# The first layer's gate, shift and scale computed by tiles of 128 features, between the phases of the second scan

## The chip, the cores and the metric

The kernel runs on one core of a Trainium2 chip. The metric is the time of one execution on the device in microseconds (us): the median of several runs. A profile is taken of one further execution; its trace has every instruction with its start, its end and what it waited for. TensorE (PE) multiplies matrices, a stationary operand being loaded first (PEld) and a moving operand then passing through; DVE, ACT and POOL work elementwise; SP issues the DMA transfers. Each engine takes its instructions in the order in which they are written for it.

## What is computed

Two layers of a diffusion backbone for 1024 latent and 128 context tokens, each 1024 wide. Each layer modulates its tokens by six vectors that are projected from a conditioning vector; there are two conditioning vectors, one for the latent and one for the context tokens.

```python
sh1, sc1, g1, sh2, sc2, g2 = jnp.split(jax.nn.silu(cvec) @ lp['w_ada'] + lp['b_ada'], 6, axis=-1)
h = rmsnorm(x, lp['g_pre_mix']) * (1.0 + sc1) + sh1
m, extras = mixing(h, lp, ctx)
x = x + g1 * rmsnorm(m, lp['g_post_mix'])
h = rmsnorm(x, lp['g_pre_ffn']) * (1.0 + sc2) + sh2
f = conv_ffn(h, lp['w_up'], lp['ffn_conv_w'], lp['ffn_conv_b'], lp['w_down'])
x = x + g2 * rmsnorm(f, lp['g_post_ffn'])
```

The change concerns three of the six parts in the first layer: part 2, the gate `g1`, and parts 3 and 4, shift `sh2` and scale `sc2` of the feed-forward sub-layer. Each is a product of two vectors of 1024 with a 1024x1024 fp32 matrix, plus a bias. `mixing` splits into a convolution module (conformer), a gated DeltaNet with four heads (two scans over nine chunks of 128 tokens, heads 0 and 1 in the first, 2 and 3 in the second) and a neighbourhood attention with four heads; their outputs are concatenated and projected.

## The kernel before

One program, written out without loops on the chip, runs layer 0 and then layer 1. In a layer it runs, in this order: the dense products of DeltaNet heads 0 and 1 and their first scan; the dense products and block inversions (line 820) of heads 2 and 3; the attention's dense products and the products of `z` (`z_dense`, line 600); the second scan, with pieces of the attention between its phases; `gdn_out` (transposes, line 998); what is left of the attention, the conformer's output (`conf_out`, lines 1067 and 1098) and the split of the output projection's weights (`out_weights`); the output projection with the next normalisation (`out_proj`, transposes on line 387); the feed-forward stage; and the normalisation for the next layer.

The six vectors are made in different places. Parts 0 and 1 of layer 0 come first of all (`ada_pe`). Part 5 of layer 0 and all six of layer 1 are made inside the feed-forward stage of layer 0 (`ada`, its products on line 241 with a 128x128 stationary operand and 64 columns). Parts 2, 3 and 4 of layer 0 are made by `ada_fill`: the stationary operand is `self.cs[:, k, :]`, two columns (the two conditioning vectors after silu), and rows of the weight matrix, 512 wide, are the moving operand (line 273). The bias comes as one more product of one row (line 278). The result lies on two partitions. For the gate it is multiplied by `g_post_mix` and written to `rows` in DRAM (lines 284 and 285), where `out_proj` reads it; for shift and scale it is copied by ACT, turned by small transposes (line 291) and copied to `mod`, features on partitions, which `turn` reads. The gate is run as a whole after the attention's dense products; shift and scale are stepped one product at a time with the rest of the attention after the second scan, from a pool `adf` of their own.

For most of the kernel a planner sets each engine's order from the order of the program, as soon as it holds an instruction to be ready. In the second scan and `gdn_out` TensorE's order is that of the program (`manual_schedule(engines=ENG)`); the other engines' is planned. `gdn_scan` runs the phases of two heads in turn and calls `fill` twice in each of nine steps; `fill` takes pieces of the attention until their stated costs reach `FILL` = 2.2:

```python
            go(0)
            if s:
                go(1)
            go(0)
            fill(s)
            go(1)
            go(0)
            go(1)
            fill(s)
```

A phase of the scan uses PSUM banks "a" and, one for each head, "b" or "c". Lines 930 (state products), 938, 949 and 951 are the scan's, 1307 (scores), 1335 (transposes, "turns") and 1351 (values) the attention's; their pieces have stated costs of 0.6, 0.55 and 0.6. Weight buffers `raw`, `whi` and `wlo` have two slots each; the attention's bias tiles of heads 0 and 2 take one slot of `whi` and of `wlo`. Line 624 loads rows that are 512 bytes long for 128 partitions, line 271 the weights of the projections.

Of the kernel before, what the change touches and what calls it, by code (L numbers as in the profile page):

```python
# [9 lines left out]
F32 = mybir.dt.float32  # L10
# [3 lines left out]
ALU = mybir.AluOpType  # L14
# [94 lines left out]
class K:  # L109
# [141 lines left out]
    def ada_fill(self, l, part, tag, both, pool=None):  # L251

        nc, I = self.nc, self.I
        def raw():
            if pool:
                return pool.tile([128, 512], F32, tag="adf", name="rawa", bufs=6)
            self.cnt += 1
            if self.cnt % 3 == 0:
                return self.wp.tile([128, 1024], F32, tag="raw", name="rawa", bufs=self.rawb)
            return self.wp.tile([128, 4 * TAIL], F32, tag=("whi", "wlo")[self.cnt % 3 - 1], name="rawa", bufs=self.wb)  # L260

        if part != 2:
            m = self.cp.tile([128, 2, KT], F32, tag=f"mod{part}", name="mod", bufs=2)
            self.mod[l, part] = m
        for ns in ((0, 1),) if both else ((0,), (1,)):
            w = 512 * len(ns)
            c0 = 512 * ns[0]
            pss = [self.psum(tag) for n in ns]
            for k in range(KT):
                r = raw()  # L270
                nc.sync.dma_start(out=r[:, :w], in_=I["w_ada"][l, 128 * k:128 * k + 128, part * D + c0:part * D + c0 + w])
                for i, ps in enumerate(pss):
                    nc.tensor.matmul(ps[0:2, :], self.cs[:, k, :], r[:, 512 * i:512 * i + 512], start=(k == 0), stop=False)  # L273
                yield
            r = raw()
            nc.sync.dma_start(out=r[0:1, :w], in_=I["b_ada"][l:l + 1, part * D + c0:part * D + c0 + w])
            for i, ps in enumerate(pss):
                nc.tensor.matmul(ps[0:2, :], self.ones[0:1, 0:2], r[0:1, 512 * i:512 * i + 512], start=False, stop=True)
            x = raw()
            if part == 2:  # L280
                nc.sync.dma_start(out=x[0:2, :w], in_=I["g_post_mix"][l:l + 1, c0:c0 + w].to_broadcast([2, w]))
                for i, ps in enumerate(pss):
                    c = slice(512 * i, 512 * i + 512)
                    nc.vector.tensor_tensor(out=x[0:2, c], in0=ps[0:2, :], in1=x[0:2, c], op=ALU.mult)
                nc.sync.dma_start(out=self.rows[l, part][:, c0:c0 + w], in_=x[0:2, :w])
            else:
                for i, (n, ps) in enumerate(zip(ns, pss)):
                    self.act(x[0:2, 512 * i:512 * i + 512], ps[0:2, :], AF.Copy)
                    for k in range(4):
                        c = 512 * i + 128 * k  # L290
                        nc.tensor.transpose(ps[:, 2 * k:2 * k + 2], x[0:2, c:c + 128], self.ident[0:2, 0:2])
                    pv = ps[:, 0:8].rearrange("p (k s) -> p s k", s=2)
                    mo = m[:, :, 4 * n:4 * n + 4]
                    if part == 4:
                        g = self.v(l, "g_pre_ffn", 4 * n, 4).unsqueeze(1).to_broadcast([128, 2, 4])
                        self.stt(mo, pv, 1.0, g, ALU.add, ALU.mult)
                    else:
                        nc.vector.tensor_copy(out=mo, in_=pv)
            yield
# [1331 lines left out]
    def run(self):  # L1631
# [23 lines left out]
        for l in range(L):  # L1655
# [53 lines left out]
            if l == 0:  # L1709
                run(self.ada_fill(0, 2, "d", True))  # L1710
# [149 lines left out]
```

## Time and profile before

| | us |
|---|---|
| median of 3 runs | 3434.82 |
| lowest and highest run | 3434.27 and 3440.16 |
| the profiled execution | 3428.76 |
| its span, first to last instruction | 3426.6 |
| TensorE busy | 3182.8 |
| DVE, ACT, POOL busy | 2094.5, 1323.0, 1151.5 |

The span is that of the traced instructions. "Busy" counts the time in which an engine has an instruction at work; matmuls overlap, so the distance between the starts of two says what one costs in a row of them. One fp32 product appears as two instructions in the trace. Rows of line numbers read: line, engine, operation, result<-operands, count, duration in ns (least, median, most), first and last start in us from the span's start.

### The profile page before, as it was taken

The numbers are of one execution on the slowest core, as the hardware profiler recorded it, in microseconds if no ns is written. First come the engines' busy times: TensorE is split into PE (matmuls) and PEld (weight loads), VectorE is DVE, ScalarE is ACT, GpSimd is POOL, SyncE is SP. The second block draws the span as 40 slices with busy tenths as digits, with TensorE's granted clock in tenths as the row PEclk, the third lists the DMA queues.
The fourth block names the chain that finished last, engine by engine and source line by source line (L and its number), as shares of the span: only waits on it lengthen the run. The fifth ranks groups of instructions, "written<-read, shape, count | busy, mean of one in ns | idle before, by whom it ended". The sixth has DMA issues, their size and how long they took to land.

```text
span 3426.6 us, 51062 instructions
## 1 busy us (share of the span) xinstructions
PE 3182.8 (93%) x19072; PEld 2874.3 (84%) x19072; DVE 2094.5 (61%) x3952; ACT 1323.0 (39%) x2987; POOL 1151.5 (34%) x1125
## 2 busy tenths in 40 slices
PE   7998888889999999999989988878799999999997
PEld 4898886737889899989978988877588999999997
DVE  3576997644566656655475769986554444444446
ACT  4335524644533333333254345246553222222223
POOL 2423223424544434434235233244342222221114
PEclk9999999999999999999999999989899999999999
DMA  5422444265322222222144224432541111111113
GB/s 190 119 64 77 139 135 127 68 221 165 108 82 83 86 72 77 87 74 71 41 141 133 68 79 139 134 93 60 178 153 45 41 43 53 43 44 38 37 37 135
DMA packets 243085, 323.78 MB, mean 94 GB/s; under 512 B 76175, under 2 KB 169631, under 8 KB 241750
## 3 DMA queue, kind: packets, MB, share of 16 engines
q1 hardware_dynamic: 242838, 320.52, 30.7%
q8 instruction: 151, 2.47, 0.3%
q14 instruction: 96, 0.79, 0.1%
HBM read 252.85 MB, written 67.59 MB: 94 GB/s over the span
## 4 chain that ended last, share of the span: by engine, by line
PE 59%; DVE 8%; DMA 4%; POOL 3%; issue 2%; ACT 2%; SPq 1%; DVEq 0%; POOLq 0%; ACTq 0%
PE d L429 18%; PE d L431 18%; PE d L430 18%; DVE cu L119 1%; PE a L930 1%; DVE adacc L119 1%; PE a L387 1%; DVE cv L119 1%; DVE XN L1625 1%; PE b L273 1%; DVE F L1626 0%; PE a L820 0%; PE S L1307 0%; PE c L241 0%; DVE keys L1626 0%
## 5 line engine op out<-in xcount | busy, mean ns | idle before, releaser
L431 PE MATMUL d<-hhi,wlo 128*128 128x386 f32 (+1 forms) x3072 | 1059.0, 345 | 14.9 <-POOL wlo L420 14.9
L429 PE MATMUL d<-hhi,whi 128*128 128x386 f32 (+1 forms) x3072 | 1055.3, 344 | 6.4 <-DVE cv L119 6.4
L430 PE MATMUL d<-hlo,whi 128*128 128x386 f32 (+1 forms) x3072 | 1055.2, 343 | 0.0
L420 POOL TENSOR_TENSOR wlo<-raw,whi 128x1024 fp32r<-128x1024 f32 x136 | 348.7, 2566 | 1064.7 <-ACT whi L116 1063.1
L119 DVE SCALAR_TENSOR_TENSOR cv<-d,fvec,cv 128x384 f32<-128x384 f32 (+1 forms) x528 | 325.3, 617 | 462.0 <-ACT cv L116 453.5
L431 PEld LDWEIGHTS d<-hhi,wlo 128*128 128x128 f32 x3072 | 585.6, 191 | 17.9 <-POOL wlo L420 16.4
L429 PEld LDWEIGHTS d<-hhi,whi 128*128 128x128 f32 x3072 | 587.6, 191 | 10.7 <-issue 8.8
L430 PEld LDWEIGHTS d<-hlo,whi 128*128 128x128 f32 x3072 | 588.0, 191 | 2.7 <-issue 0.7
L1539 DVE TENSOR_TENSOR f<-d,f 128x512 f32<-128x512 f32 x360 | 245.1, 687 | 163.7 <-PE d L431 161.9
L116 ACT ACTIVATE cv<-d,fvec 128x384 f32<-128x384 f32 (+1 forms) x264 | 174.7, 663 | 439.9 <-PE d L431 431.4
L429 PE MATMUL d<-wdh,ahi 128*128 128x512 f32 x792 | 315.6, 398 | 10.9 <-DVE f L1539 8.4
L430 PE MATMUL d<-wdl,ahi 128*128 128x512 f32 x792 | 313.4, 396 | 0.0
L431 PE MATMUL d<-wdh,alo 128*128 128x512 f32 x792 | 312.5, 395 | 0.0
L119 DVE SCALAR_TENSOR_TENSOR cu<-cu,vec 128x292 f32<-128x292 f32 (+1 forms) x480 | 248.2, 559 | 1.9
L116 ACT ACTIVATE whi<-raw 128x1024 fp32r<-128x1024 f32 x136 | 144.2, 1060 | 175.7 <-PE d L430 124.3
L223 POOL TENSOR_TENSOR adacc<-adacc,adpr 128x512 f32<-128x512 f32 x112 | 152.6, 1362 | 125.4 <-ACT adpr L116 94.8
L429 PEld LDWEIGHTS d<-wdh,ahi 128*128 128x128 f32 x792 | 149.0, 188 | 50.0 <-DVE f L1539 13.1
L1526 POOL TENSOR_TENSOR wdl<-rawd,wdh 128x512 fp32r<-128x512 f32 x88 | 118.7, 1349 | 184.3 <-ACT wdh L116 183.8
L431 PEld LDWEIGHTS d<-wdh,alo 128*128 128x128 f32 x792 | 148.7, 188 | 36.1 <-issue 0.7
L430 PEld LDWEIGHTS d<-wdl,ahi 128*128 128x128 f32 x792 | 148.9, 188 | 34.4 <-issue 1.4
L116 ACT ACTIVATE adpr<-adraw,cs 128x512 f32<-128x512 f32 x112 | 81.0, 723 | 240.9 <-POOL adacc L223 191.5
L1515 DVE TENSOR_TENSOR alo<-sg,ahi 128x384 fp32r<-128x384 f32 x132 | 110.8, 840 | 69.5 <-ACT ahi L116 69.2
(381 smaller groups left out, 5199.1 us busy)
## 6 DMA issues: line engine op xcount, KB each, us to landing
raw<-in_w_up_t SPq DMA_DIRECT2D x88, 512.0 KB
adraw<-in_w_ada SPq DMA_DIRECT2D x112, 256.0 KB
raw<-in_w_in_t SPq DMA_DIRECT2D x48, 512.0 KB
rawd<-in_w_down SPq DMA_DIRECT2D x88, 256.0 KB
xs<-x SPq DMA_DIRECT2D x27, 512.0 KB
x<-xs SPq DMA_DIRECT2D x27, 512.0 KB
rawa<-in_w_ada SPq DMA_DIRECT2D x24, 512.0 KB
x<-in_x SPq DMA_DIRECT2D x18, 512.0 KB
```

The source lines that it names most:

```text
L116: return self.nc.scalar.activation(out=out, in_=in_, func=func, **kw)
L119: return self.nc.vector.scalar_tensor_tensor(out=out, in0=in0, scalar=s, in1=in1, op0=op0, op1=op1, **kw)
L223: nc.gpsimd.tensor_tensor(out=acc[:, 1, :], in0=acc[:, 1, :], in1=pr, op=ALU.add)
L273: nc.tensor.matmul(ps[0:2, :], self.cs[:, k, :], r[:, 512 * i:512 * i + 512], start=(k == 0), stop=False)
L387: nc.tensor.transpose(ps[:, 128 * k:128 * k + 128], xn[:, 512 * g + 128 * k:512 * g + 128 * k + 128], self.ident)
L420: nc.gpsimd.tensor_tensor(out=lo[:, :n], in0=raw[:, :n], in1=hi[:, :n].bitcast(F32), op=ALU.subtract)
L429: nc.tensor.matmul(out, shi, mhi, start=(i == 0), stop=False)
L430: nc.tensor.matmul(out, shi, mlo, start=False, stop=False)
L431: nc.tensor.matmul(out, slo, mhi, start=False, stop=(i == n - 1))
L1515: nc.vector.tensor_tensor(out=lo[:, :n], in0=sg[:, :n], in1=hi[:, :n].bitcast(F32), op=ALU.subtract)
L1526: nc.gpsimd.tensor_tensor(out=lo, in0=raw[:, :512], in1=hi[:].bitcast(F32), op=ALU.subtract)
L1539: nc.vector.tensor_tensor(out=f[t][:, cs], in0=ps, in1=f[t][:, cs], op=ALU.add)
```

## The change

`ada_fill` goes and `ada_cols` takes its place. For each tile of 128 output features it loads all 1024 rows of 128 columns of the weight matrix (`r`, in runs of 512 bytes), makes them the stationary operand, eight 128x128 blocks one after another, and lets the two columns of `self.cs` pass. The result has features on partitions; ACT adds the bias and writes one column for each conditioning vector into `mod`. Loads run three tiles ahead (`la`). The gate is turned once at the end, multiplied by `g_post_mix` and written to `rows`; the scale gets its `g_pre_ffn` at its end. The generator has 25 steps: 24 tiles, and the turn of the gate. The run of the gate ahead of the second scan is taken out. In the second scan of layer 0 `fill` takes one step from its third call on, once its pieces have passed half of `FILL`, and counts it as 0.8; the steps use bank "c" in one call and "b" in the next. What is left of the steps is taken with the rest of the attention as before; the pool `adf` is gone.

```diff
--- before.py
+++ after.py
@@ -248,55 +248,48 @@
                     nc.vector.tensor_copy(out=m, in_=pv)
             yield
 
-    def ada_fill(self, l, part, tag, both, pool=None):
+    def ada_cols(self, l, parts, la=3):
 
         nc, I = self.nc, self.I
+
         def raw():
-            if pool:
-                return pool.tile([128, 512], F32, tag="adf", name="rawa", bufs=6)
             self.cnt += 1
             if self.cnt % 3 == 0:
                 return self.wp.tile([128, 1024], F32, tag="raw", name="rawa", bufs=self.rawb)
-            return self.wp.tile([128, 4 * TAIL], F32, tag=("whi", "wlo")[self.cnt % 3 - 1], name="rawa", bufs=self.wb)
-
-        if part != 2:
-            m = self.cp.tile([128, 2, KT], F32, tag=f"mod{part}", name="mod", bufs=2)
-            self.mod[l, part] = m
-        for ns in ((0, 1),) if both else ((0,), (1,)):
-            w = 512 * len(ns)
-            c0 = 512 * ns[0]
-            pss = [self.psum(tag) for n in ns]
+            return self.wp.tile([128, 4 * TAIL], F32, tag=("whi", "wlo")[self.cnt % 3 - 1], name="rawa", bufs=self.wb)[:, :1024]
+
+        def load(part, j):
+            r = raw()
+            c0 = part * D + 128 * j
+            nc.sync.dma_start(out=r[:].rearrange("p (k c) -> p k c", c=128), in_=I["w_ada"][l, :, c0:c0 + 128].rearrange("(k p) c -> p k c", p=128))
+            return r
+
+        todo = [(part, j) for part in parts for j in range(KT)]
+        rs = [load(*x) for x in todo[:la]]
+        for i, (part, j) in enumerate(todo):
+            if j == 0:
+                m = self.cp.tile([128, 2, KT], F32, tag=f"mod{part}", name="mod", bufs=2 if part != 2 else 1)
+                self.mod[l, part] = m
+            r = rs.pop(0)
+            ps = self.psum(self.adt)
             for k in range(KT):
-                r = raw()
-                nc.sync.dma_start(out=r[:, :w], in_=I["w_ada"][l, 128 * k:128 * k + 128, part * D + c0:part * D + c0 + w])
-                for i, ps in enumerate(pss):
-                    nc.tensor.matmul(ps[0:2, :], self.cs[:, k, :], r[:, 512 * i:512 * i + 512], start=(k == 0), stop=False)
+                nc.tensor.matmul(ps[:, 0:2], r[:, 128 * k:128 * k + 128], self.cs[:, k, :], start=(k == 0), stop=(k == KT - 1))
+            self.act(m[:, :, j], ps[:, 0:2], AF.Identity, bias=self.v(l, "b_ada", 8 * part + j))
+            if i + la < len(todo):
+                rs.append(load(*todo[i + la]))
+            if j == KT - 1 and part == 4:
+                for s in range(2):
+                    self.stt(m[:, s, :], m[:, s, :], 1.0, self.v(l, "g_pre_ffn", 0, KT), ALU.add, ALU.mult)
+            yield
+            if j == KT - 1 and part == 2:
+                ps = self.psum(self.adt)
+                nc.tensor.transpose(ps[0:16, 0:128], m[:].rearrange("p s k -> p (s k)"), self.ident)
+                g = raw()[0:16, 0:128]
+                for s in range(2):
+                    nc.sync.dma_start(out=g[8 * s:8 * s + 8, :], in_=I["g_post_mix"][l].rearrange("(k c) -> k c", c=128))
+                nc.vector.tensor_tensor(out=g, in0=ps[0:16, 0:128], in1=g, op=ALU.mult)
+                nc.sync.dma_start(out=self.rows[l, 2].rearrange("s (k c) -> (s k) c", c=128), in_=g)
                 yield
-            r = raw()
-            nc.sync.dma_start(out=r[0:1, :w], in_=I["b_ada"][l:l + 1, part * D + c0:part * D + c0 + w])
-            for i, ps in enumerate(pss):
-                nc.tensor.matmul(ps[0:2, :], self.ones[0:1, 0:2], r[0:1, 512 * i:512 * i + 512], start=False, stop=True)
-            x = raw()
-            if part == 2:
-                nc.sync.dma_start(out=x[0:2, :w], in_=I["g_post_mix"][l:l + 1, c0:c0 + w].to_broadcast([2, w]))
-                for i, ps in enumerate(pss):
-                    c = slice(512 * i, 512 * i + 512)
-                    nc.vector.tensor_tensor(out=x[0:2, c], in0=ps[0:2, :], in1=x[0:2, c], op=ALU.mult)
-                nc.sync.dma_start(out=self.rows[l, part][:, c0:c0 + w], in_=x[0:2, :w])
-            else:
-                for i, (n, ps) in enumerate(zip(ns, pss)):
-                    self.act(x[0:2, 512 * i:512 * i + 512], ps[0:2, :], AF.Copy)
-                    for k in range(4):
-                        c = 512 * i + 128 * k
-                        nc.tensor.transpose(ps[:, 2 * k:2 * k + 2], x[0:2, c:c + 128], self.ident[0:2, 0:2])
-                    pv = ps[:, 0:8].rearrange("p (k s) -> p s k", s=2)
-                    mo = m[:, :, 4 * n:4 * n + 4]
-                    if part == 4:
-                        g = self.v(l, "g_pre_ffn", 4 * n, 4).unsqueeze(1).to_broadcast([128, 2, 4])
-                        self.stt(mo, pv, 1.0, g, ALU.add, ALU.mult)
-                    else:
-                        nc.vector.tensor_copy(out=mo, in_=pv)
-            yield
 
     def ada_pool(self, pool, tag):
         shapes = {"raw": ([128, 512], 2), "pr": ([128, 512], 1), "acc": ([128, 2, 512], 1)}
@@ -1706,8 +1699,6 @@
             zs = chain(*(self.z_dense(l, h, hh, gc) for h in (2, 3)))
             for i in range(2):
                 self.attn_dense(l, i, hh, gc)
-            if l == 0:
-                run(self.ada_fill(0, 2, "d", True))
             with self.tc.high_priority(-LOW):
                 self.conf_conv(l, range(NCV, 8), pcp)
             for _ in range(ZA):
@@ -1724,13 +1715,25 @@
                 yield from self.attention(l, ap, right.enter_context(P("psat", space=PSUM)), first)
 
             att = pieces()
+            ads = iter(())
+            if l == 0:
+                ads = self.ada_cols(0, (2, 3, 4))
+            turn = []
+
             def fill(s):
-                c = 0.0
+                c, left = 0.0, True
+                turn.append(0)
+                self.adt = "bc"[len(turn) % 2]
                 while c < FILL:
                     x = next(att, None)
                     if x is None:
                         return
                     c += x
+
+                    if left and c > 0.5 * FILL and len(turn) > 2:
+                        left = False
+                        if next(ads, self) is not self:
+                            c += 0.8
 
             with self.tc.manual_schedule(engines=ENG):
                 o23 = self.gdn_scan(l, heads, S, sc, fill)
@@ -1747,9 +1750,7 @@
                 W = []
                 ws = self.out_weights(l, wpool, W)
                 mid = ExitStack()
-                if l == 0:
-                    adp = mid.enter_context(P("adf"))
-                ads = chain(*(self.ada_fill(0, part, "b", False, adp) for part in (3, 4) if l == 0))
+                self.adt = "b"
                 co = self.conf_out(l, mid.enter_context(P("conv")))
                 for i, _ in enumerate(att):
                     next(ads, None)
```

## Rows read from the trace of the kernel before

**Rows 1.** The page: busy time by engine; the chain that ended last.

```profile
PE 3182.8 (93%) x19072; PEld 2874.3 (84%) x19072; DVE 2094.5 (61%) x3952; ACT 1323.0 (39%) x2987; POOL 1151.5 (34%) x1125
...
PE 59%; DVE 8%; DMA 4%; POOL 3%; issue 2%; ACT 2%; SPq 1%; DVEq 0%; POOLq 0%; ACTq 0%
```

**Rows 2.** Lines on PE; of each pair layer 0, then layer 1.

```profile
L820 PE MATMUL a<-room,DA x144: 184/191/213, 513.2 to 521.8; 32*32 32x32 f32 x144
...
L820 PE MATMUL a<-room,DA x144: 191/220/258, 2231.1 to 2246.5; 32*32 32x32 f32 x144
...
L930 PE MATMUL a<-S,kq x128: 271/275/580, 582.0 to 676.8; 128*128 128x128 f32 x128
...
L930 PE MATMUL a<-S,kq x128: 270/275/582, 2285.2 to 2387.0; 128*128 128x128 f32 x128
...
L998 PE MATMUL c<-ident,on x18: 273/327/332, 691.6 to 709.5; 128*128 128x128 f32 x18
...
L998 PE MATMUL c<-ident,on x18: 272/328/332, 2401.8 to 2419.7; 128*128 128x128 f32 x18
...
L387 PE MATMUL a<-ident,xn x72: 270/273/421, 797.0 to 892.0; 128*128 128x128 f32 x72
...
L387 PE MATMUL a<-ident,xn x72: 270/273/473, 2481.6 to 2576.0; 128*128 128x128 f32 x72
```

**Rows 3.** The tile `rawa` (weights of the projections): its products and transposes.

```profile
L273 PE MATMUL b<-rawa,cs x64: 589/592/1061, 718.5 to 770.4; 128*2 128x512 f32 x64
...
L273 PE MATMUL d<-rawa,cs x32: 591/592/593, 521.9 to 549.9; 128*2 128x512 f32 x32
...
L291 PE MATMUL b<-ident,rawa x16: 195/198/263, 738.3 to 773.5; 2*128 2x2 f32 x16
```

**Rows 4.** PE timeline: start us, us, engine line op, merged count; two bursts.

```profile
521.92 1.88 PE L273 MATMUL d<-rawa,cs 128*2 128x512 f32 x4
...
1044.58 1.89 PE L241 MATMUL c<-ones,adacc 128*128 128x64 f32 x16
```

**Rows 5.** PE timeline of one round of the second scan, layer 0.

```profile
636.16 1.16 PE L930 MATMUL a<-S,kq 128*128 128x128 f32 x8
...
638.41 0.42 PE L1307 MATMUL S<-kh,q 128*128 128x384 f32 x1
...
639.02 0.62 PE L1335 MATMUL P<-ident,SX 128*128 128x128 f32 x4
639.57 0.54 PE L1351 MATMUL P<-PT,V 128*64 128x128 f32 x5
...
640.16 0.44 PE L1307 MATMUL S<-kh,q 128*128 128x384 f32 x1
```

**Rows 6.** Line 930 on PE, layer 1, 2305 to 2395.

```profile
L930 PE MATMUL a<-S,kq x112: 270/275/582, 2308.9 to 2387.0; 128*128 128x128 f32 x112
```

**Rows 7.** PE's waits, layer 1, 2305 to 2402: total us, times, longest.

```profile
PE P L1335 <- DVE PT L1337: 3.4, 3, 1.1
PE P L1325 <- ACT ov L116: 3.0, 2, 1.6
PE c L938 <- DVE ty L119: 2.0, 1, 2.0
```

**Rows 8.** Stretches of PE, layer 1: us, busy, granted clock, DMA share, GB/s.

```profile
2420.00:2430.00 10.00, 4.79 (x31) 0.86 0.93 322
2430.00:2440.00 10.00, 2.50 (x8) 0.50 0.33 108
2440.00:2450.00 10.00, 5.94 (x19) 0.50 0.40 120
```

**Rows 9.** A stretch, layer 0: PE, PEld, DVE, ACT, POOL busy, clock, DMA.

```profile
660.00:670.00 10.00, 6.95 (x42) 5.66 (x41) 5.90 (x18) 6.58 (x26) 0.86 (x1) 0.83 0.31 79
```

**Rows 10.** SP timeline: DMA issues, start us, us, count.

```profile
112.34 7.93 SPq L624 DMA_DIRECT2D E<-gT  x4
...
520.13 7.23 SPq L271 DMA_DIRECT2D rawa<-in_w_ada  x5
```

## The prediction

> **What bounds the kernel now.** I read the page first, then the timeline by layer. On the page [rows 1] TensorE is busy for 93% of the span and carries 59% of the chain that ended last: matmul time in a stage counts unless that stage has gaps on TensorE. The change touches layer 0 only, and layer 1 runs the same stages without these three projections, because the second layer's come out of `ada` inside the feed-forward stage. So layer 1 is a measurement of layer 0 without them. I cut both layers at four marks, each the first or last start of a line [rows 2]: the first product of the block inversion before the second scan (L820), the first state product of that scan (L930), the last transpose of `gdn_out` (L998), the last transpose of the output projection (L387).
>
> - A, L820 to L930: 513.2 to 582.0 = 68.8 us in layer 0, 2231.1 to 2285.2 = 54.1 us in layer 1.
> - B, L930 to L998: 582.0 to 709.5 = 127.5 us against 2285.2 to 2419.7 = 134.5 us.
> - C, L998 to L387: 709.5 to 892.0 = 182.5 us against 2419.7 to 2576.0 = 156.3 us.
>
> Together 378.8 against 344.9 us: the three projections cost layer 0 at present 33.9 us. The gate lies in A (+14.7), shift and scale in C (+26.2), and B is 7.0 shorter in layer 0, since there the attention's first loads are out earlier relative to the scan.
>
> **What the work itself costs on TensorE.** Each fp32 product is two instructions in the trace. Now: 32 instructions for the gate and 64 for shift and scale, 512 columns wide over a two-column stationary operand [rows 3]. Four of them take 1.88 us with a last one of 0.592 [rows 4], so (1.88 - 0.592) / 3 = 0.429 us apart: 96 x 0.429 = 41.2 us. The bias rows are 6 more products of the same width, 12 x 0.429 = 5.1 us, and the 16 transposes are at most 16 x 0.2 = 3.2 us [rows 3]. Sum 46 to 50 us, of which the gate has 15.5 (14.7 of it seen in A, so it is almost wholly exposed) and shift and scale 34.
>
> After: 24 tiles of 8 products = 16 instructions, each with its own 128x128 fp32 stationary load and two moving columns. The trace has no such pair. Nearest is L241: 128x128 fp32 stationary, 64 columns, 16 of them in 1.89 us, the last 0.275 [rows 4]: (1.89 - 0.275) / 15 = 0.108 us apart. I take 0.108, so a tile is 16 x 0.108 = 1.72 us and all 24 are 41.4 us. From below, no row shows a 128x128 pair closer than that. From above, L930's longest instruction is 580 against a median of 275 ns at the lower clock [rows 2], so 0.22 us; that is a rival below. The 24 bias additions move into the ACT copy. TensorE's own work thus falls by 5 to 9 us only. What decides is how much of the 41 us is hidden at the new places.
>
> The Trainium skill ("TensorE: Matmul & The Clock Gate", section Back-to-back issue gap) puts a matmul of 1 to 64 columns at an issue floor of about 25 ns; by that a tile would be 0.4 us, an estimate, and the forecast some 30 us lower. The same page's section LDWEIGHTS has the load go by columns, 128 / 1.2 = 107 ns, and L241's 0.108 us sides with the load.
>
> **A, the gate taken out.** `run(self.ada_fill(0, 2, "d", True))` goes, with 8 loads of 512 KB, 36 instructions and 2 multiplies. TensorE was full there, so layer 0 should take layer 1's 54.1 us: -14.7.
>
> **B, sixteen tile steps in the scan.** TensorE's order is written by hand here, so I counted `fill` by its constants. Now a call takes about four attention pieces (2.35). After, from the third call on, it takes a score piece, a turn piece, one tile step and a value piece, and stops. One round without a stall reads [rows 5]: scan phases 636.16 to 638.41 = 2.25 us, score 0.61, turn 0.55, value 0.59. With the tile: 2.25 + 0.61 + 0.55 + 1.72 + 0.59 = 5.72 us. Layer 1's rounds start from 2308.9 to 2387.0 in 14 groups of 8 [rows 6]; less the last group's own 0.8 that is 77.3 / 13 = 5.95 us a round, stalls included. So a tile fits into about the time of a stalled round. Thirteen unstalled rounds are 13 x 5.72 = 74.4 us. Of the waits [rows 7] the 3.4 us of turns for the PT copies go, since a round then has one turn and not two; 3.0 and 2.0 us stay, and I allow 2 for the smaller ones: 81.4, or +4.1 over layer 1. The two last calls carry the context pieces and a tile, by the constants 7.0 instead of 4.7: +2.3. Two new waits: the PSUM bank ("b" or "c") of the scan head just finished, whose last DVE readers must be done, and the first load. Neither is seen before; I bound them by 0 (a score and a turn piece, 1.16 us, lie between) and 0.5 us in each of 16 rounds, and take 1.6. Queued behind a waiting tile on TensorE are a value piece and the other head's scan phase. B becomes 134.5 + 8 = 142.5 us, between 134.5 (tiles cover all remaining waits) and 150.5.
>
> The loads move onto SP's queue past the attention's own. Each is 512 KB in 512-byte runs. The nearest rows [rows 10]: four loads of 576 KB in 512-byte runs held SP for 7.93 us, 2.0 each, and five present loads in 4 KB runs 7.23 us, 1.4 each. One load a round of 5.7 us, three ahead, is covered; if it were not, each would cost a round up to 2 us.
>
> **C, the tail.** Nine tiles remain, 9 x 1.72 = 15.5 us. The scan also took fewer attention pieces, so by the constants 15.95 instead of 7.1 remain here: +8.85. Against layer 1 that is 24.4 us more TensorE work. Cover: layer 1's TensorE is busy for 4.79 + 2.50 + 5.94 = 13.2 of the 30 us from 2420 to 2450 [rows 8], while the conformer output and the split of the output weights go through DVE, ACT and POOL, so up to 16.8 us can be hidden. The present code hid 34 - 26.2 = 8 us in the same gap. Between 8 and 16.8 I take 12.3: C = 156.3 + 12.1 = 168.4 us, between 163.9 and 180.7. What is late next is the output projection's first token tile, which needs the attention's last head.
>
> **Sum.** 54.1 + 142.5 + 168.4 = 365.0 against 378.8: -13.8 us. Nothing else changes in layer 0 or 1. Best ends: 54.1 + 134.5 + 163.9, -26.3; worst ends: 54.1 + 150.5 + 180.7, +6.5. The profiled execution took 3428.76 us (span 3426.6) and so would come to 3415.0; it is 6 us under the median of the runs, 3434.82. From the median: 3421.0 us, ends 3408.5 and 3441.3.
>
> **Rivals.**
> 1. Slower: the clock. A tile is 1.72 us of loads with hardly any columns moving, in each round. TensorE's granted clock in the scan is not always full: 660 to 670, with 6.95 us busy of 10, had 0.83 [rows 9], and the gap of layer 1 after its attention had 0.50 [rows 8]. If the loads don't count as activity, stretches of the scan fall to 1.2 GHz. Sixteen rounds are 92 us; at a mean of 0.75 they would take 92 / 0.75 - 92 = 31 us more: 3452 us. The gain is used up when the mean falls to 0.87 (13.8 us) and the kernel is over 0.2% slower from 0.82. Against it: the rest of each round, 4.0 us, is dense. What the Trainium skill ("TensorE: Matmul & The Clock Gate", Part 1) says is only that the gate follows how busy the array was; whether weight loads count is not said there, and no run here shows it.
> 2. No gain: the waits. If the tiles' loads, bank or buffer slots (whi and wlo each give one to the attention's bias tiles) hold the in-order TensorE for 0.5 us in each of 24 steps, and the tail hides no more than today's 8 us, 13.8 shrinks by 12 + 4: about 3437 us.
> 3. Better: everything is covered, both waits and tail gap: 3408 us or a little under.
>
> **How the numbers follow.** Forecast 0.55 (3412 to 3432), better 0.12, no gain 0.15, clock 0.18. A measurement of this kernel tells about 0.2%, 6.9 us, from no change. Faster by more: 0.55 + 0.12, less 0.05 for the forecast's upper end, 0.62; within: 0.05 + 0.15, 0.20; slower: the clock, 0.18. The likeliest is 3421.0. The range goes from 3404 (below the best ends, as a tile could be cheaper than L241's) to 3450, which takes in the worst ends and the milder half of the clock rival.
>
> **What would show it.** Right: L820 to L930 near 54 us; tile instructions 0.11 us apart; rounds near 5.7 us, hardly any wait of turns for PT; L998 to L387 near 168 us with little idle on TensorE. Wrong: tile instructions 0.21 apart and a granted clock well under 0.9 in the scan (rival 1); idle ahead of the tiles, ended by a DMA or by DVE's readers of "b" and "c" (rival 2); A still near 69 us; rounds of over 6.5 us at full clock.

## The result, and the profile after

The changed kernel takes 3467.55 us, median of 6 runs (3459.74 to 3477.34), the kernel before 3436.24 us beside it: a ratio of 1.0094, interval 1.0082 to 1.0105. It is 31.3 us slower. 3421.0 was forecast, and the range ended at 3450. The profiled execution has a span of 3460.7 us.

The page of after, answering [rows 1]: busy time of TensorE, the clock granted to it in 40 slices, the chain.

```profile
PE 3205.6 (93%) x19333; PEld 2938.0 (85%) x19333; DVE 2096.4 (61%) x3949; ACT 1327.7 (38%) x3007; POOL 1158.8 (33%) x1125
...
PEclk9999998868999999999999999999899999999999
...
PE 58%; DVE 8%; POOL 3%; DMA 3%; ACT 3%; issue 3%; SPq 1%; DVEq 0%; POOLq 0%; ACTq 0%
```

TensorE is busy 22.8 us longer, although its own work should have fallen. The clock row dips to 8, 8, 6 and 8 in slices 7 to 10 (519 to 865 us): layer 0's second scan and what follows. Before, it read:

```profile
PEclk9999999999999999999999999989899999999999
```

The four marks in layer 0, answering [rows 2]. Lines above the change's own have moved up by 7: L820 is L813, L930 is L923, L998 is L991, L387 is L380.

```profile
L813 PE MATMUL a<-room,DA x144: 191/218/258, 516.7 to 531.2; 32*32 32x32 f32 x144
...
L923 PE MATMUL a<-S,kq x128: 273/275/582, 569.7 to 683.0; 128*128 128x128 f32 x128
...
L991 PE MATMUL c<-ident,on x18: 270/307/476, 717.1 to 740.3; 128*128 128x128 f32 x18
...
L380 PE MATMUL a<-ident,xn x72: 270/273/474, 835.0 to 927.9; 128*128 128x128 f32 x72
```

A is 569.7 - 516.7 = 53.0 us (forecast 54.1), B 740.3 - 569.7 = 170.6 (142.5), C 927.9 - 740.3 = 187.6 (168.4). The sum is 411.2 where 365.0 was forecast and 378.8 stood before. The same two stretches B and C as windows, first before, then after (columns: us, PE busy with its instructions, granted clock, DMA share, GB/s):

```profile
582.00:709.50 127.50, 105.82 (x832) 0.93 0.38 96
709.50:892.00 182.50, 163.74 (x695) 0.96 0.58 184
```

```profile
569.70:740.30 170.60, 151.27 (x1072) 0.82 0.51 126
740.30:927.90 187.60, 160.47 (x752) 0.86 0.49 153
```

The clock fell from 0.93 to 0.82 and from 0.96 to 0.86. Inside the scan, in steps of 10 us:

```profile
600.00:610.00 10.00, 9.60 (x71) 0.83 0.43 108
610.00:620.00 10.00, 9.11 (x60) 0.74 0.21 56
620.00:630.00 10.00, 9.38 (x59) 0.67 0.47 129
...
670.00:680.00 10.00, 10.00 (x91) 1.00 0.09 12
...
700.00:710.00 10.00, 9.88 (x47) 0.50 0.52 94
```

From 700 to 710 TensorE is busy for 9.88 of 10 us and yet has 1.2 GHz (0.50) throughout. So this doesn't look like the clock of an idle engine, as in [rows 8]. Idle time in B (170.6 - 151.3 = 19.3 us) is even 2.4 us less than before (21.7).

A round where nothing goes wrong, on PE's timeline; its clock is 1.00, while the earlier part of 660 to 670 has less. It answers [rows 5]:

```profile
664.89 1.16 PE L923 MATMUL a<-S,kq 128*128 128x128 f32 x8
...
667.75 0.62 PE L1328 MATMUL P<-ident,SX 128*128 128x128 f32 x4
668.21 1.92 PE L276 MATMUL c<-cs,rawa 128*128 128x2 f32 x16
670.06 0.54 PE L1344 MATMUL P<-PT,V 128*64 128x128 f32 x5
...
670.65 0.60 PE L923 MATMUL a<-S,kq 128*128 128x128 f32 x3
```

It lasts 670.65 - 664.89 = 5.76 us (forecast 5.72). Its tile's 16 instructions are (1.92 - 0.25) / 15 = 0.111 us apart, 0.25 being the middle duration in the rows of the tile `rawa`:

```profile
L276 PE MATMUL b<-cs,rawa x272: 167/251/374, 601.1 to 773.3; 128*128 128x2 f32 x136
L276 PE MATMUL c<-cs,rawa x112: 170/251/353, 594.9 to 697.1; 128*128 128x2 f32 x112
```

What PE waited for from 590 to 718 (total us, times, longest):

```profile
PE c L931 <- DVE rawa L290: 4.3, 1, 4.3
PE b L276 <- DVE o L961: 2.0, 3, 0.9
...
PE c L276 <- DVE o L961: 1.1, 2, 0.6
```

The second and third are the wait for the PSUM bank, foreseen at 0 to 0.5 us a round and taken at 1.6: together 3.1 us. The first was not foreseen. The gate's closing step multiplies by `g_post_mix` on VectorE, and the loads of that factor go out 4.6 us after the gate has been turned (L286, at 652.49). On SP's and DVE's timelines:

```profile
657.14 0.63 SPq L289 DMA_DIRECT2D rawa<-in_g_post_mix  x2
```

```profile
659.28 0.28 DVE L290 TENSOR_TENSOR rawa<-c,rawa 16x128 f32<-16x128 f32 x1 [2.60 <-DMA rawa<-in_g_post_mix]
```

The scan's next product into bank "c" (L931) waits for that multiply. One more stall stands in C: 9.25 us ahead of a product of the output projection, whose split factor `chi` is late because the loads it needs stood on SP's queue behind the conformer's stores (`cat<-yh`):

```profile
818.55 0.80 PE L422 MATMUL d<-rhi,chi 128*128 128x512 f32 x1 [9.25 <-ACT chi L116]
```

```profile
806.68 4.14 SPq L1102 DMA_DIRECT2D cat<-yh  x4
812.52 0.61 SPq L1436 DMA_DIRECT2D oc<-ot  x1
```

So two theories stood after the result. **N**: the narrow products. A tile moves two columns a product, and TensorE, though busy, gets the lower clock for it; that makes B and C long. **W**: the waits (bank, late factor, loads) lengthen the rounds, and the clock falls as a consequence of the idle time.

### The profile page after: what moved, and what is told of

The parts are those of the page before. It is cut to its first block, busy times and chain, and to the rows that moved or that the text cites. A ratio compares the mean times of both kernels' runs of the same rounds, so it can differ in the third digit from the quotient of the medians.

```text
span 3460.7 us, 51584 instructions
## 1 busy us (share of the span) xinstructions
PE 3205.6 (93%) x19333; PEld 2938.0 (85%) x19333; DVE 2096.4 (61%) x3949; ACT 1327.7 (38%) x3007; POOL 1158.8 (33%) x1125
## 4 chain that ended last, share of the span: by engine, by line
PE 58%; DVE 8%; POOL 3%; DMA 3%; ACT 3%; issue 3%; SPq 1%; DVEq 0%; POOLq 0%; ACTq 0%
PE d L422 17%; PE d L423 17%; PE d L424 17%; DVE cu L119 2%; DVE cv L119 1%; PE a L923 1%; DVE adacc L119 1%; POOL adacc L223 1%; POOL hlo L363 1%; PE a L380 0%; PE a L813 0%; POOL wlo L413 0%; PE P L1344 0%; PE a L942 0%; PE c L241 0%
## 5 line engine op out<-in xcount | busy, mean ns | idle before, releaser
L422 PEld LDWEIGHTS d<-hhi,whi 128*128 128x128 f32 x3072 | 587.7, 191 | 11.5 <-issue 9.9
L424 PEld LDWEIGHTS d<-wdh,alo 128*128 128x128 f32 x792 | 148.7, 188 | 36.2 <-issue 0.7
```

The source lines that it names most:

```text
L422: nc.tensor.matmul(out, shi, mhi, start=(i == 0), stop=False)
L424: nc.tensor.matmul(out, slo, mhi, start=False, stop=(i == n - 1))
```

## The experiments

In all the tables, A, B and C are the stages of layer 0 in the profiled execution, us. A second profile of the kernel before, taken to see how well these repeat:

> The kernel before, unchanged, for a second profile of it. The first one ran 6 us below the median of its runs. If the stages repeat (68.8 / 127.5 / 182.5 us within 2 each), stage sums of two profiles can be set against each other to 2 us; if they move by more than that with the stretches at the lower clock, only the timed runs resolve differences of a few us, and the stages show where, not how much.

It gave 69.0 / 122.6 / 185.2, sum 376.8 against 378.8: the sum repeats to 2 us here, a single stage only to 5. Differences of a few us are therefore read from the timed runs, and the stages only show where. The rest of the span, outside the three stages and written alike in all kernels, moves as well: 3426.6 - 378.8 = 3047.8 us in the first profile, 3433.5 - 376.8 = 3056.7 in the second.

**More columns, the same places.** Each product gets 64 columns (first kernel) or 128 (second), by repeating the two of `cs`; ScalarE reads one column of each half. The first:

```diff
-                nc.tensor.matmul(ps[:, 0:2], r[:, 128 * k:128 * k + 128], self.cs[:, k, :], start=(k == 0), stop=(k == KT - 1))
+                nc.tensor.matmul(ps[:, 0:64].rearrange("p (s w) -> p s w", s=2), r[:, 128 * k:128 * k + 128], self.cs[:, k, :].unsqueeze(2).to_broadcast([128, 2, 32]), start=(k == 0), stop=(k == KT - 1))
...
```

> As the changed kernel, but each of the tile's products lets 64 columns pass instead of 2 (each conditioning vector read 32 times); the 128x128 loads, the waits and the order stay. Theory N (narrow products): a burst of loads with two columns each hardly counts as activity of TensorE, the granted clock falls (mean 0.82 in stage B of the changed kernel, 171 us), and everything in the scan and the tail runs at 1.2 GHz for a good part. Then 64 columns bring the mean in B to 0.92 or more, B to 145-152 us, and the kernel to 3425-3445 us. Theory W (waits): the clock falls because TensorE stands idle ahead of the tiles (bank, loads). Then the clock and the time stay as in the changed kernel, 3460-3475 us. By both, tile instructions stay 0.108 to 0.113 us apart at full clock.

> As before, with 128 columns for each product (each conditioning vector read 64 times). Theory N: at least as high a clock as with 64 columns (0.93 or more in B), and a time within 5 us of that run, since at 128 columns the instructions are 0.112 us apart (as the scan's own). Theory W: 3460-3475 us, clock in B near 0.82.

Measured: 64 columns 3437.29 us, ratio 0.9999 (0.9983 to 1.0016), stages 54.2 / 147.7 / 180.8; 128 columns 3430.86 us, ratio 0.999 (0.9977 to 1.0003), stages 52.8 / 150.2 / 170.9. B and C of the 128-column kernel:

```profile
565.10:715.30 150.20, 130.45 (x1028) 0.92 0.56 142
715.30:886.20 170.90, 152.59 (x793) 0.96 0.54 168
```

The clock is back at 0.92 and 0.96, and 36.7 of the kernel's us with it (3467.55 - 3430.86; by the two ratios some 36), though the tiles' multiply-adds on TensorE are now 64 times as many. The bank waits are all still there:

```profile
PE c L276 <- DVE o L961: 1.9, 3, 0.8
PE b L276 <- DVE o L961: 1.6, 3, 0.8
```

At 3.5 us they are no smaller than the 3.1 of the changed kernel. N's time and B came out, W's did not; N's clock was missed by 0.01 each time (0.91 with 64 columns, 0.92 with 128), and the two kernels lie 6.4 us apart where it said 5. Two other waits of the changed kernel are gone with the low clock, though: the 4.3 us for the late factor (its loads now go out at 634.08, ahead of the gate's turn at 641.32) and the 9.25 us for `chi`. So this pair alone doesn't part the clock from those two; the ladder and the old places below do. And C varies by itself: with 64 columns it took 180.8 us at a clock of 0.90, without the stall for `chi`.

**Fewer narrow products.** One product of eight in each tile, so that 7/8 of the contraction is left out:

```diff
-            for k in range(KT):
-                nc.tensor.matmul(ps[:, 0:2], r[:, 128 * k:128 * k + 128], self.cs[:, k, :], start=(k == 0), stop=(k == KT - 1))
+            for k in (0,):
+                nc.tensor.matmul(ps[:, 0:2], r[:, 128 * k:128 * k + 128], self.cs[:, k, :], start=(k == 0), stop=True)
```

> Each tile makes one of its eight products only, so seven eighths of the contraction of gate, shift and scale are left out; loads, bank waits, ACT copies and the order of everything else stay. Theory N: with 0.2 instead of 1.8 us of narrow products in a round the clock stays up (0.93 or more in B), and B is 135-142 us, the kernel 3405-3425 us. Theory W: waits for banks, loads and the gate's product remain and hold the clock down: B over 150 us, kernel over 3440 us.

Measured: 3422.46 us, ratio 0.9965 (0.995 to 0.998), stages 54.3 / 136.0 / 181.8, clock in B 0.90. N's B and time came out, its clock (0.93) did not, and W's B and time did not. So with a tile at an eighth of its price the kernel gains 0.35%, some 12 us (7 to 17 by the interval): about the 13.8 that I forecast for whole tiles. It is no strict ceiling: the products that remain are still narrow, and the kernel has both long waits of the changed one, 4.5 us for the late factor and 9.2 of the 12.0 us for `chi`. Its clock in C is 0.87 although hardly any narrow products are left there; TensorE idles there for 33.6 of the 181.8 us.

**The gate alone in the scan**, shift and scale by the old rows of 512 columns behind it:

```diff
-                ads = self.ada_cols(0, (2, 3, 4))
+                ads = self.ada_cols(0, (2,))
...
-                self.adt = "b"
+                run(ads)
+                if l == 0:
+                    adp = mid.enter_context(P("adf"))
+                ads = chain(*(self.ada_fill(0, part, "b", False, adp) for part in (3, 4) if l == 0))
```

> Only the gate goes by tiles in the scan (nine steps); shift and scale are made after the scan as in the kernel before, with 512 columns to a product. Theory N: the clock is lost in the first half of the scan only, B is 148-155 us, and C comes back to the 182 us of before or a little above for the attention that is left over; kernel 3440-3450 us. Theory W as to C (the tail is long because attention and tiles delay the conformer's output and the loads queued on SP behind it): C stays near 188 us even without the tiles, as the attention that is left over stays for the most part.

Measured: 3444.56 us, ratio 1.0025 (1.0009 to 1.0042), stages 52.6 / 142.3 / 192.0, clock in B 0.88 and in C 0.94. With 8 narrow tiles the kernel is 0.25% slower, with 24 it is 0.94%. That fits N in the time alone. By its stages N missed twice: B is 142.3 us and not 148 to 155, and C, where no narrow products stand, is 192.0 and not 182, longer even than W's 188. So the loss of this kernel lies in C, and the run doesn't show that narrow products cause it.

**The clock by itself.** A ladder of products ahead of the kernel before, each over a 128x128 fp32 load, one after the other with nothing to wait for:

```diff
+                for n, count in ((512, 40), (2, 100), (512, 40), (64, 100), (512, 40), (128, 100), (512, 40)):
...
+                    for i in range(count):
+                        nc.tensor.matmul(lps[:, 0:n], wide[:, 128 * (i % 4):128 * (i % 4) + 128], wide[:, 0:n], start=True, stop=True)
```

> The kernel before with a ladder of products at its very start, and nothing else changed: over the same 128x128 fp32 loads 40 products of 512 columns, 100 of 2, 40 of 512, 100 of 64, 40 of 512, 100 of 128, 40 of 512, in this order on TensorE, with no wait between them. Its time is before's with the ladder on top and isn't compared; what is read is the granted clock in each block. Theory N (products with few columns don't keep the clock up): in the block of 2 columns, 200 instructions of some 0.11 us or 22 us, the granted clock falls to 0.50 although TensorE is never idle, and it is back at 1.00 in the block of 512 behind it; in the blocks of 64 and 128 columns it falls less or not at all. Theory W (the clock fell in the changed kernel since TensorE waited there): no block waits, so the clock is 1.00 in all of them but the first. If 64 columns hold 1.00 and 2 don't, what was wrong in the changed kernel is the column count by itself.

Six stretches of PE, inside the blocks of 512, 2, 512, 64, 512 and 128 columns:

```profile
25.00:54.00 29.00, 29.00 (x69) 1.00 0.10 32
58.00:94.00 36.00, 36.00 (x171) 0.50 0.00 0
99.00:130.00 31.00, 31.00 (x73) 1.00 0.00 1
131.00:153.00 22.00, 22.00 (x200) 1.00 0.00 1
154.00:187.00 33.00, 33.00 (x78) 1.00 0.00 0
188.00:210.00 22.00, 22.00 (x199) 1.00 0.00 1
```

This settles it apart from everything else in the kernel. TensorE is busy for every microsecond, hardly any DMA moves after the first block, and with 2 columns it has 1.2 GHz (0.50), with 64, 128 or 512 it has 2.4 (1.00). An instruction with 2 columns then takes 36.00 / 171 = 0.211 us, with 64 it takes 22.00 / 200 = 0.110, with 128 the same 22.00 / 199 = 0.111. The wide one is the cheaper one. The multiply-adds that are thrown away cost no time here: 64 columns take as long as 128.

**Place and form apart.** The first kernel has tiles of 128 columns at the old places (gate ahead of the scan, shift and scale in the tail, none in the scan); the second the same with 2 columns.

```diff
+            if l == 0:
+                self.adt = "d"
+                run(self.ada_cols(0, (2,)))
             with self.tc.high_priority(-LOW):
...
-                ads = self.ada_cols(0, (2, 3, 4))
+                ads = self.ada_cols(0, (3, 4))
...
-                    if left and c > 0.5 * FILL and len(turn) > 2:
+                    if False:
```

> Tiles of 128 features with 128 columns a product, at the places of the kernel before: the gate ahead of the second scan, shift and scale with the attention's rest behind it, none in the scan. Place theory (what the change can win lies in the rounds of the scan, where a tile takes some of TensorE's waits away): this kernel gains nothing on before, stages 68 / 128 / 182 us, sum 378 within 4, time within 4 us of before, and some 4 to 5 us above the 128-column kernel in the scan (sum 373.9). Form theory (the tiles are cheaper than the rows of 512 wherever they stand, 8 x 16 x 0.113 = 14.5 us against the 15.7 us that stage A lost with the gate): some 1 us less in each part, sum 375, time 3 us below before, and the scan is worth about nothing. Displacement theory (putting them in the scan costs by the rounds' stretched waits): sum below 372, faster than the 128-column kernel in the scan.

> The tiles at the old places (gate ahead of the second scan, shift and scale with the attention's rest behind it), with 2 columns a product as in the changed kernel, in place of 128. The kernel with 128 columns there was at 0.9966 of before (3424 us). Clock theory (products of 2 columns lower the granted clock wherever several tiles stand close together, whatever work is around them): the granted clock falls to 0.50 in parts of the stretch ahead of the scan and in the tail, where tiles follow at 2.3 us from each other, low time in stages A and C rises by 15 us or more, and the time is 8 us or more above the 128-column one, 3432 or more. Scan theory (2 columns hurt only in the scan, whose other products are small too): the clock is as in the 128-column one and the time within 4 us of it.

Measured: 128 columns 3424.48 us, ratio 0.9966 (0.9954 to 0.9978); 2 columns 3463.66 us, ratio 1.0077 (1.0065 to 1.0089). The gate's tiles and 10 us among them, in the 128-column kernel:

```profile
L276 PE MATMUL d<-cs,rawa x128: 273/275/582, 527.2 to 558.2; 128*128 128x128 f32 x128
```

```profile
537.00:547.00 10.00, 9.90 (x184) 1.00 0.38 108
```

The same two of the 2-column kernel:

```profile
L276 PE MATMUL d<-cs,rawa x128: 352/353/374, 525.5 to 562.7; 128*128 128x2 f32 x128
```

```profile
537.00:547.00 10.00, 10.00 (x150) 0.50 0.07 19
```

With 2 columns not one of the 128 instructions had the full clock: the shortest took 352 ns, against 251 as the middle one in the scan. The clock theory's marks were all reached. By stages the 2-column kernel has 81.6 / 152.7 / 180.0 us, sum 414.3, at clocks of 0.73, 0.85 and 0.83; the 128-column one 41.4 / 160.7 / 178.6, sum 380.7, at 0.88, 0.93 and 0.94. Neither has a stall of over 2 us for `chi` or one of TensorE for a late factor, and the columns are all that the two programs differ in. So the narrow form costs about the same at either place, 36.7 us in the scan and 39.2 here (some 36 and 38 by the ratios), and the place matters little:

| columns | in the scan | old places |
|---|---|---|
| 2 | 1.0094 (1.0082 to 1.0105) | 1.0077 (1.0065 to 1.0089) |
| 128 | 0.9990 (0.9977 to 1.0003) | 0.9966 (0.9954 to 0.9978) |

The 128-column kernel at the old places is the best full version measured: it is 12.3 us faster than before (3436.78 beside it). Of its theories the displacement one came out on the time, but not on the stages: it asked for a sum of less than 372, the kernel has 380.7, and the 128-column kernel in the scan had 373.9. (A and B can't be set beside the other kernels' one by one: the scan's first product stands at 558.3 here, ahead of the products of `z`, and the next ones at 599.0. Together they are 202.1 us, 196.3 before.) A second look at it:

> The 128-column tiles at the old places once more, for a second profile. Its first one ran 6 us above the median of its runs and its stages (41.4 / 160.7 / 178.6, sum 380.7) don't show the 12 us by which the timed runs are under before. Clock theory: at a profile near its median 3424 the sum is 370 to 375, with less low time. Else the sum stays near 380 and the gain lies outside of these stages.

The stages came out the same (41.3 / 160.2 / 179.0, sum 380.5), and the run was at 3431.69 us against 3437.68 for the kernel before. Both profiled executions lie over 7 us above the median of this kernel's timed runs, so they need not hold the 12 us. Their stages don't; where the gain lies stays open. The place is judged by the timed runs alone.

**The bank wait.** As the 128-column kernel in the scan, but with the tile behind the round's value piece:

```diff
-                while c < FILL:
+                step = 0.8 if ads_left and len(turn) > 2 else 0.0
+                while c < FILL - step:
                     x = next(att, None)
...
+                if step and next(ads, self) is self:
+                    ads_left.clear()
```

> As the 128-column kernel, but a round's tile stands behind that round's pieces of the attention in place of between them, and a round makes room for it beforehand (0.8 of its budget). Bank theory (the tile's first product waits for VectorE to read the bank of an earlier round's piece, 1.9 + 1.6 us in the 128-column kernel's stage B, and its piece waits behind it): the wait goes, stage B 150.3 to some 147, C as it was, time 3 to 4 us below the 128-column kernel. Work theory (stage B is longer by TensorE's own work): B 150 within 1.5, time within 2 us of the 128-column kernel.

Measured: 3430.16 us, ratio 0.9977 (0.9965 to 0.9989), stages 54.1 / 148.7 / 172.2. The waits of L276 from 590 to 718:

```profile
PE b L276 <- ACT mod L116: 2.6, 1, 2.6
...
PE c L276 <- DVE o L961: 0.5, 1, 0.5
```

The bank's wait shrank from 3.5 us to 0.8 (0.5 here and 0.3 on "b"), and a wait for a copy of `mod` came, once, 2.6 us. B fell by 1.5, which is within what the work theory allows and not the bank theory's 3; by the ratios the time is some 4 us lower, more than the work theory's 2, but the intervals of the two kernels overlap, so no gain on the time is shown. The wait for the bank is real, and with 128 columns it is 3.5 us in all.

**The displaced pieces.** As the 128-column kernel, with the tile not counted in the round's budget:

```diff
-                        if next(ads, self) is not self:
-                            c += 0.8
+                        next(ads, None)
```

> As the 128-column kernel, but a tile isn't counted in a round's budget, so that no piece of the attention is put off to the tail for it. The forecast priced what is put off at 8.9 us in stage C. Displacement theory: B rises by 8 to 10 us (150.3 to some 159), C falls by as much (170.9 to some 162), the sum of 373.9 and the time stay within 2 us. Cover theory (in the scan these pieces fall into waits of TensorE, in the tail they don't): B rises by less than 6, C falls by 9, and the time is 3 us or more below the 128-column kernel. Wait theory (longer rounds run into the waits of the chain of the scan): B rises by more than 12, and the time is 3 us or more above it.

Measured: 3433.38 us, ratio 0.9989 (0.9977 to 1.0), stages 54.1 / 162.9 / 166.9. B and C:

```profile
569.50:732.40 162.90, 138.38 (x1100) 0.92 0.57 143
732.40:899.30 166.90, 149.87 (x721) 0.90 0.53 161
```

B rose by 12.7 us, C fell by 4.0 at a lower clock (0.90 against 0.96), and the ratio is the same to 0.0001. No theory came out whole: B is the wait theory's, the time the displacement theory's. The stages' sum rose by 10.0 us, to 383.9, which the timed runs don't bear out. By them, work that is put off from the scan to the tail is neither gained nor lost within their intervals.

**Only shift and scale in the scan**, the gate at its old place, 128 columns (the kernel with the tiles at the old places, its `if False` taken back to the condition of the changed one):

> 128 columns a product; the gate at its old place ahead of the second scan, shift and scale by tiles between the phases of the scan. With all three in the scan the time was 0.9977 to 0.999 of before (3430 us), with none there 0.9966 (3424 us). Gate theory (what the scan costs over the old places comes with the gate: its multiply waits 4.3 us for its late factor, and its stretch ahead of the scan was half idle): at 0.9966 or below, 3424 within 3 us or faster. Place theory (each tile in a round lengthens the round and puts pieces of the attention off): two thirds of the difference, 3428 within 2 us. Tail theory (what is dear is that shift and scale stand in the way of conf_out and the attention's rest): faster than 3420.

Measured: 3434.65 us, ratio 0.9994 (0.9985 to 1.0003). All three theories missed: it is level with all three in the scan (0.9990), and not between that and none. The gate theory falls, since the kernel is no faster with the gate out of the scan. (Its 4.3 us for the late factor were the changed kernel's; with 128 columns that wait wasn't there to be saved.) Against none in the scan (0.9966) the 16 tiles of shift and scale cost 0.28%, and the gate's 8 on top nothing that shows. Why they cost that is not settled.

## Why the prediction was wrong

**The step that failed is the clock: the sum has no term for it, and rival 1, which has one, is wrong in its chance, its price and the argument against it.** The loads with few columns did not keep the clock up, as that rival said, and I gave it 0.18, since "the rest of each round, 4.0 us, is dense". The ladder shows that 2-column products lower the clock with TensorE fully busy, and the scan's clock fell to 0.67 over 10 us of rounds that have that dense rest. The rival had "over 0.2% slower from 0.82", and B's mean was 0.82, but the result was 0.94% slower. It was priced over the 92 us of the rounds alone; C, which fell to 0.86, was not in it. Setting the changed kernel beside the 128-column one splits the loss: 170.6 - 150.2 = 20.4 us in B, 187.6 - 170.9 = 16.7 in C, 37.1 in all, and 36.7 by the timed runs. By their windows, TensorE is busy 151.27 - 130.45 = 20.8 us longer in B and 160.47 - 152.59 = 7.9 in C: the same products in the two stages together, at the lower clock. The other 8.8 us of C are idle time; the stall for `chi` would account for them. Its cause is open. A late end of B isn't needed for it: the kernel with one product in eight has the stall too, 9.2 us, after a B of 136.0. Nor is C's share a fixed price: against the 64-column kernel it is 187.6 - 180.8 = 6.8 us, and at the old places 2 columns cost C 1.4. With 37.1 the forecast of -13.8 becomes +23.3, and with the 8.9 us of the sizes below +32.2; the result was +31.3. That is the stages' difference taken apart, not a second measurement of it.

**Right, by its own steps.** A: 53.0 us for 54.1. The tile: 0.111 us an instruction at the full clock, for 0.108 taken from a row of the same load with 64 columns. That row hid the point, though: it was right in duration and said nothing of what 2 columns do to the clock. The round: 5.76 us for 5.72; and from the first state product of the first round to that of the last, the 13 rounds took 81.0 us in the 128-column kernel (584.5 to 665.6), for the 81.4 worked out, and 75.9 in the kernel without the bank wait (587.7 to 663.6), for the 74.4 without any stall. That 81.0 and 81.4 agree is partly luck: the 7 us of stalls that I allowed aren't in it, since TensorE idles for 3.65 us from 584.5 to 671.6, about the bank's 3.5. In the changed kernel the rounds took 93.0 (589.1 to 682.2). Turns waiting for PT do not appear in the list of waits from 590 to 718. No tile of the changed kernel waited for its load (one of the 128-column kernel did, in C, 3.4 us).

**Sizes.** The bank wait was 3.1 us for 1.6. The gate's factor, 4.3 us, was missed: I counted its tiles and not the DMA that its closing step issues, and L931 is queued behind that step's bank. The 128-column kernel, with the gate at the same place, doesn't wait for it; why its loads went out in time there is open. In C I let the tail hide 12.3 us of 24.4 us of new work. With 128 columns, C was 170.9 us for 168.4. TensorE idled there for 170.9 - 152.6 = 18.3 us, and the same stretch of layer 1 before for 25.4 by its window:

```profile
2419.70:2576.00 156.30, 130.90 (x608) 0.91 0.51 160
```

So 7.1 us were hidden, less than the 8 to 16.8 that I allowed. B with 128 columns was 7.7 us over its 142.5. Most of it is my mark: 18 of the 24 tiles began ahead of the last transpose (L991) there, and I counted 15 (16 steps, one of them the gate's turn); three tiles of 1.8 us are 5.4. In the changed kernel 20 did. Sum: 373.9 for 365.0, the 8.9 above.

**The larger error behind it.** I asked what of the 33.9 us could be hidden. The table shows that the move hides nothing measurable even when the clock is not lowered: 0.9990 in the scan, 0.9966 at the old places. Rounds of the scan were not free. In layer 1 before, TensorE was busy for 66.2 of their 77.3 us:

```profile
2308.10:2385.40 77.30, 66.22 (x524) 0.91 0.34 73
```

So a tile of 1.8 us in each round lengthens them or puts attention pieces off, and the kernel that let them lengthen came out level. The gain that is there, 0.34%, came with 128-column tiles at the old places; how the form brings it is not shown, since the stages don't hold it.

The Trainium skill ("TensorE: Matmul & The Clock Gate", section Back-to-back issue gap) has a floor of about 25 ns for a 2-column matmul by itself, and says that in a stream of loads and matmuls both set the distance. The ladder's 0.110 us for 64 and 128 columns alike sides with the load by columns of the Trainium skill's section LDWEIGHTS (same page; 107 ns for 128), as the forecast did; at a clock of 0.50 the measured 0.211 us is twice that. Part 1 of the same page of the Trainium skill ties the clock to how busy the array was. The trace agrees for mostly idle stretches [rows 8]; the ladder shows TensorE busy without a gap and at 0.50.

## What to carry to other kernels

Where a load goes with each product, look at the columns and not only at the duration: at full clock an instruction with 2 columns took as long as one with 128, 0.11 us, but a row of them had half the clock, and so had work behind them. Try the moving operand repeated to 64 or 128 columns, and read only what is needed. Before moving work into a loop "between phases", add up TensorE's busy time in that loop's rounds; here it was 66.2 of 77.3 us, and the move hid nothing measurable. When a forecast takes a duration from a row with another shape, ask what else that shape changes.

## What the runs showed of the hardware

A TensorE that was busy without a gap did not keep the full clock. Products of 2 columns over 128x128 fp32 loads, without a gap, ran at 1.2 GHz (0.50) from 58 to 94 us, at 0.211 us an instruction; products of 64 and 128 columns at 2.4 GHz, 0.110 and 0.111. More multiply-adds, 32 to 64 times as many, took half the time. The low clock also outlasted its cause: the last instruction of the ladder's 2-column block began at 94.6 us, and the clock was 0.50 through all of 85 to 98, so wide products behind the block ran at it too.
